# Up projection on fp16 halves with one scale taken in the mLSTM, the next unit's first products inside a unit, and down sums made by adding transfers

## The chip, the core and the metric

One Trainium2 chip, one of its cores. The core's engines are TensorE (PE; its weight loads are listed as PEld), VectorE (DVE), ScalarE (ACT), GpSimd (POOL) and SyncE (SP), which only issues transfers. The metric is the device time of one launch in microseconds (us). Each engine works through its own instructions in a fixed order; an instruction whose wait is not yet met holds everything behind it on that engine.

## The reference

One layer with two token mixers and a convolutional feed-forward block, in float32, for 1024 latent tokens of width 1024 and 256 context tokens:

```python
h  = modulate(rms_norm(x, norm1_w), sh1, sc1)           # and the same for ctx
q,k,v, mq,mk,mv,mo,mg, ga,gm = split(h @ w_in)
att = windowed_gqa(q, k, v, k_ctx, v_ctx, attn_sink)    # 16 heads, window 128, all context keys
ml  = mlstm_readout(mlstm_bidirectional(...), mo)       # 4 heads, chunks of 128, both directions
y   = sigmoid(ga) * (att @ w_branch_att) + sigmoid(gm) * (ml @ w_branch_ml)
x_mid = x + g1 * (y @ w_out)
u   = modulate(rms_norm(x_mid, norm2_w), sh2, sc2) @ w_up          # 1024 -> 2 * 2816
a,g = split(conv_b + depthwise conv of width 3 over tokens of u)
out = x_mid + g2 * ((silu(g) * a) @ w_down)                        # 2816 -> 1024
```

## The kernel before, in words

**Stages.** In the profiled execution the attention with its projections runs to about 560 us, the mLSTM (`stage_mlstm`) to about 955 us, the tail (`stage_tail`: branch products, the output projection `project`, the second norm, transposes, operand sums) to about 1208 us, the up projection in 22 units (`Units`, called from `stage_ffn`) to about 1636 us, and the down projection from there to the end.

**Halves.** A product of two float32 operands is made as three TensorE products of halves, high by high, high by low, low by high (`product`, L2023 to L2029; `mm3`, L163 to L165). `split_from` (L50) makes the halves: ACT copies the source to the high half (L47), DVE subtracts the high half from the source (L54, without a scale, or L56, with one). In the attention and mLSTM projections the halves are fp16 and the weights carry a scale; in the tail, up and down stages they are fp32r, 4 bytes an element. A TensorE instruction of the up stage multiplies a 128x128 block into a 128x512 bank of PSUM.

**The scheme with seven products.** The up and down projections use a Strassen-like scheme: seven products of quarter matrices instead of eight, with sums of quarters as operands. Of the activations `stage_tail` makes seven operands, `b11 b21 t2 t1 t3 b22 t4` (`put`). Of the weights, each unit j of 128 + 128 channels loads one 1 MB tile `ur` (`lead`), sums its quarters on DVE (`prep`, `prep2`) and splits them into pairs `r1 q1 q2 r2`. A product is 4 blocks x 3 = 12 TensorE instructions, a unit 7 products = 84, all 22 units 1848.

**Order of a unit.** `first_mm(j)` makes the two products that need only `r1`; `rest(j)` makes the other five and leaves two results `ua` and `ug`, which `conv_gate` (ACT and DVE) turns into a tile `a` of hidden channels and SP stores to `f_d` in DRAM. Unit j's operands are prepared during unit j-1.

**Sums for the down projection.** `weight_sums(k)` loads four 256 KB blocks of `w_down`, makes four subtractions on DVE and stores four blocks to `wt_d`: three of the eleven k in the tail (loads on ACT's queue, L1939, subtractions L1906), the others one per unit in the first half of the up stage. `hidden_sums(k)` runs in the second half: it loads a stored tile `fa` back, makes four operations on DVE with the present one and stores 512 KB each to `s1_d` and `s2_d`.

**The mLSTM's end.** `readout` squares the head's output on ACT, POOL makes the factor `rr` (L1520, and a power in L1521), DVE scales `hf` (L1524), TensorE transposes it (`mt`, L1532), and DVE multiplies by the gate (`mo`, L1534). The TensorE products that run meanwhile are those of the output gate (also named `mo`, operands `hH`/`hL` and `whqo`/`wlqo`). After that the branch product `yb` begins.

**Norm in the tail.** For each of the 8 row blocks of `x_mid`, `square` takes ACT squares, DVE adds them (L1873) and POOL raises them to a power (`rrx`, L1874); `scale` (L1877) multiplies the block, and transposes (`x2p`, L1913) read it.

**What sets the order.** Each engine's static order is laid down at build time from the program order, the tiles' dependences and a few `issue_after` marks. DMA issues stand in the order of the engine that issues them, with the same blocking rule.

## Time and profile before

| | |
|---|---|
| median of 3 runs (lowest, highest) | 1846.55 us (1845.82, 1847.97) |
| profiled execution, its time | 1849.14 us |
| its span on the core | 1847.4 us |
| mean granted TensorE clock | 0.988 |
| busy: PE, DVE, ACT, POOL | 1790.8, 1425.9, 1069.8, 508.3 us |
| moved | 342.47 MB, mean 185 GB/s |

"Busy" counts the union of an engine's instructions. A row of the timeline reads: start, duration, engine, line, operation, out<-in, shape, and in brackets how long the engine was idle before it and what ended that. A row of the table by stretches gives for each engine busy us and the number of instructions, then the granted clock, the DMA engines' mean busy share and GB/s.

### The profile page before, as it was taken

What the parts mean: (1) busy time and instruction counts of PE and PEld (TensorE: products, weight loads), DVE (VectorE), ACT (ScalarE), POOL (GpSimd) and SP (SyncE); (2) the same over time, 40 slices, a digit from 0 to 9 for tenths busy, and PEclk for the clock granted to TensorE, in tenths of its full rate; (3) what the DMA queues carried; (4) which work ended last, traced back from release to release, by engine and by line L of the source; (5) the groups of instructions that cost most, each with busy time, mean ns of one, the idle gap of its engine ahead of it and who ended that gap; (6) DMA issues with size and microseconds to landing.
All of it is one profiled execution on the core that took longest, in us unless ns stands there. A gap on an engine that the chain in (4) does not pass through costs nothing.

```text
span 1847.4 us, 27864 instructions
## 1 busy us (share of the span) xinstructions
PE 1790.8 (97%) x9207; PEld 1283.5 (69%) x9207; DVE 1425.9 (77%) x2864; ACT 1069.8 (58%) x2229; POOL 508.3 (28%) x747
## 2 busy tenths in 40 slices
PE   7989999999998899999999999999999999999999
PEld 3855555555554566656668887878888888888887
DVE  3858888888788686858687787698889898897665
ACT  4747877878787565645356462476444444465441
POOL 2467769587862530303010020000000000000000
PEclk9999999999999899999999999999999999999999
DMA  9747988888796625261359927322454544599751
GB/s 342 233 138 146 201 170 179 192 180 199 147 182 131 219 79 192 79 213 37 132 188 368 344 92 246 141 77 106 172 207 180 194 160 166 195 318 371 260 172 69
DMA packets 302193, 342.47 MB, mean 185 GB/s; under 512 B 176208, under 2 KB 200672, under 8 KB 299232
## 3 DMA queue, kind: packets, MB, share of 16 engines
q1 hardware_dynamic: 287648, 314.47, 56.3%
q10 hardware_dynamic: 14400, 26.22, 4.2%
q8 instruction: 72, 1.18, 0.3%
q14 instruction: 73, 0.60, 0.1%
HBM read 224.61 MB, written 76.16 MB: 163 GB/s over the span
## 4 chain that ended last, share of the span: by engine, by line
PE 78%; DVE 7%; DMA 4%; issue 3%; ACT 3%; POOL 3%; SPq 0%; ACTq 0%; DVEq 0%; POOLq 0%
PE g L706 8%; PE pq L706 6%; PE pa L2027 4%; PE pa L2029 4%; PE pa L2028 4%; PE po L706 3%; PE dx L2029 2%; PE dx L2027 2%; PE dx L2028 2%; PE pb L2027 2%; PE pb L2029 2%; PE pb L2028 2%; PE yb L2029 2%; PE yb L2027 2%; PE yb L2028 2%
## 5 line engine op out<-in xcount | busy, mean ns | idle before, releaser
L850 DVE CUSTOM_DVE_ANT_0 s<-s,maskA,nsink 128x640 f32<-128x640 f32 (+1 forms) x128 | 117.4, 917 | 65.5 <-PE s L845 65.0
L866 DVE TENSOR_TENSOR P<-s,P 128x640 f16<-128x640 f32 (+1 forms) x128 | 100.6, 786 | 1.0 <-ACT s L861 1.0
L860 ACT ACTIVATE P<-s,st 128x640 f16<-128x640 f32 (+1 forms) x128 | 98.2, 767 | 4.1
L706 PE MATMUL g<-hH,fh 128*128 128x512 f16 x256 | 97.1, 379 | 0.0
L706 PE MATMUL g<-hH,fl 128*128 128x512 f16 x256 | 97.0, 379 | 0.0
L706 PE MATMUL g<-hL,fh 128*128 128x512 f16 x256 | 97.0, 379 | 0.0
L861 ACT ACTIVATE s<-s,st 128x640 f32<-128x640 f32 (+1 forms) x128 | 93.8, 733 | 0.0
L706 PEld LDWEIGHTS <-hH 128*128 128x128 f16 x640 | 62.8, 99 | 37.3 <-issue 1.8
L858 ACT ACTIVATE st<-st,shift 128x1 f32<-128x1 f32 x128 | 37.6, 294 | 85.6 <-DVE st L850 84.8
L706 PE MATMUL pq<-wha,hH 128*128 128x384 f16 (+1 forms) x256 | 84.9, 332 | 0.1
L706 PE MATMUL pq<-wha,hL 128*128 128x384 f16 (+1 forms) x256 | 84.9, 332 | 0.0
L706 PE MATMUL pq<-wla,hH 128*128 128x384 f16 (+1 forms) x256 | 84.9, 332 | 0.0
L706 PEld LDWEIGHTS <-fh 128*128 128x128 f16 x512 | 49.2, 100 | 45.4
L2165 ACT ACTIVATE cv<-ua,vecT 128x1024 f32<-128x1024 f32 x22 | 27.4, 1246 | 84.9 <-DVE ua L2138 84.9
L1436 POOL TENSOR_SCALAR kwh<-k,gcall 128x128 fp32r<-128x128 f32 x72 | 32.5, 455 | 157.2 <-PE dC L164 53.9
L47 ACT ACTIVATE dfh<-drf 128x512 fp32r<-128x512 f32 x55 | 34.4, 628 | 59.3 <-PE dx L2028 26.5
L2027 PE MATMUL dx<-dwh,dfh 128*128 128x512 f32 (+1 forms) x176 | 68.3, 388 | 0.0
L2029 PE MATMUL dx<-dwh,dfl 128*128 128x512 f32 (+1 forms) x176 | 68.2, 388 | 0.0
L2028 PE MATMUL dx<-dwl,dfh 128*128 128x512 f32 (+1 forms) x176 | 68.2, 387 | 0.0
L54 DVE TENSOR_TENSOR dfl<-drf,dfh 128x512 fp32r<-128x512 f32 x55 | 37.6, 688 | 36.1 <-ACT dfh L47 36.1
L165 PE MATMUL kv<-whkv,hL 128*128 128x384 f16 x192 | 62.6, 326 | 0.0
L164 PE MATMUL kv<-wlkv,hH 128*128 128x384 f16 x192 | 62.6, 326 | 0.0
(691 smaller groups left out, 6249.9 us busy)
## 6 DMA issues: line engine op xcount, KB each, us to landing
ur<-in_w_up SPq DMA_DIRECT2D x22, 1024.0 KB
wmb<-in_w_modB SPq DMA_DIRECT2D x48, 256.0 KB
f_d<-cv SPq DMA_DIRECT2D x22, 512.0 KB
wm<-in_w_modA SPq DMA_DIRECT2D x16, 512.0 KB
fr<-in_w_g SPq DMA_DIRECT2D x32, 256.0 KB
drf<-fs_d SPq DMA_DIRECT2D x15, 512.0 KB
drw<-wt_d SPq DMA_DIRECT2D x14, 512.0 KB
w1b<-in_w_cx SPq DMA_DIRECT2D x16, 388.0 KB
```

Source lines behind the costliest of these rows:

```text
L54: rest = nc.vector.tensor_tensor(lo, src, whole, op=ALU.subtract)
L164: nc.tensor.matmul(ps, lh[:, ls], rl[:, rs], start=False, stop=False)
L165: nc.tensor.matmul(ps, ll[:, ls], rh[:, rs], start=False, stop=stop and i == n - 1)
L706: nc.tensor.matmul(self.ps, x, w, start=self.i == 0, stop=self.i == self.n - 1)
L850: nc.vector.tensor_tensor_reduce(e, e, self.mask, scale=self.ss[:, h : h + 1], scalar=nsink[:, hh : hh + 1], op0=ALU.add, op1=ALU.min, acc ...
L858: nc.scalar.activation(m, st4[:, 8 + h : 9 + h], AF.Identity, bias=shift)
L860: nc.scalar.activation(two[:, :W], e, AF.Exp, bias=m, scale=-1.0)
L861: nc.scalar.activation(e, e, AF.Exp, bias=m, scale=-1.0, accum_out=st4[:, 4 + h : 5 + h])
L866: nc.vector.tensor_tensor(two[:, W : 2 * W], self.e[h], two[:, :W], op=ALU.subtract)
L2027: nc.tensor.matmul(ps, lh, rh, start=start and i == 0, stop=False, skip_group_check=True)
L2028: nc.tensor.matmul(ps, lh, rl, start=False, stop=False, skip_group_check=True)
L2029: nc.tensor.matmul(ps, ll, rh, start=False, stop=stop and i == n - 1, skip_group_check=True)
```

## The change

Four things are done.

1. **fp16 halves.** The operands of the up products (`r1 q1 q2 r2` and the seven activation operands) become fp16, high and low half in one tile of the size that one fp32r half had (`xpair`, `pair4`, `pair2`). All weight pairs take one scale, `E.upf[:, 2:3]`, so the ACT copy has a per-partition scale and the DVE subtraction becomes the form of L56.
2. **The scale.** It is made from the sum of squares of the whole `w_up`. During the mLSTM, ACT issues 44 loads of 512 KB (128x1024, three buffers) and squares each with an accumulated sum (`up_load`, `up_square`); after the last head's output gate `up_scales` adds them up over partitions with one TensorE product, and takes reciprocals and powers on DVE and POOL. It also takes in `norm_factors` from the tail, and scales the modulation and the convolution weights in `m2` and `vecT` by the inverse factors.
3. **Order in a unit.** `rest(j, new, between)` makes the first two products of unit j+1 inside unit j, and calls `prep` and `prep2` of unit j+1 between products. A unit's weights are loaded two units ahead.
4. **Down sums.** `weight_sums` makes no DVE operation: POOL issues loads of `w_down` blocks that add into the tile on arrival, ten transfers per k, two k at a time, 110 in all; the three early sums in the tail and their ACT loads go. `hidden_sums` makes one DVE subtraction per unit; for the first eleven units SP writes three tiles to `s1_d` and `s2_d`, for the last eleven POOL adds to them in DRAM with two transfers each. Signs of the second eleven channel groups are flipped, and `finish` and the last additions subtract accordingly.

```diff
+    def up_load():
+        n = UP["load"]
+        if n < NUP:
+            raw = UP["raw"][n] = upp.tile([P, 4, 256], F32, tag="up", name=f"um{n}")
+            nc.scalar.dma_start(raw, A["w_up"][n // 2][:, 4 * (n % 2) : 4 * (n % 2) + 4])
+            UP["load"] += 1
+    def up_square(k):
+        for _ in range(k):
...
+                nc.scalar.activation(raw, raw, AF.Square, accum_out=E.up[:, n : n + 1])
+                UP["done"] += 1
+                up_load()
+    def up_scales():
+        f, g, m2, vecT = E.upf, E.upf[:, 8:], E.m2[:, 1:3], E.vecT
...
+        nc.tensor.matmul(pb[:, : NUP + 2], E.ones, E.up[:, : NUP + 2], start=True, stop=True)
+        nc.vector.tensor_reduce(f[:, 0:1], pb[:, :NUP], axis=AX.X, op=ALU.add)
+        nc.vector.tensor_scalar(g[:, 2:4], pb[:, NUP : NUP + 2], 1.0, 1e-30, op0=ALU.mult, op1=ALU.add)
+        nc.gpsimd.tensor_scalar(f[:, 1:2], f[:, 0:1], 2.0 ** -28, 1e-36, op0=ALU.mult, op1=ALU.add)
+        nc.gpsimd.tensor_tensor(f[:, 2:3], f[:, 1:2], expo[:, 0:1], op=ALU.pow)
+        nc.gpsimd.tensor_tensor(g[:, 4:5], g[:, 2:3], expo[:, 0:1], op=ALU.pow)
...
+        nc.gpsimd.tensor_tensor(f[:, 3:4], g[:, 4:5], expo[:, 0:1], op=ALU.pow)
+        nc.vector.reciprocal(f[:, 4:6], f[:, 2:4])
...
@@ proj_kv
+            if h and j >= NCB:
+                up_square(1)
@@ proj_q
+            if h:
+                up_square(2 if h == MLH - 1 else 1)
@@ proj_o
+                if h < MLH - 1:
+                    up_square(1)
+        if h == MLH - 1:
+            up_scales()
@@ stage_tail
-            B[m][k] = [x512(f"{m}{x}{k}", pool=homes[m]) for x in "hl"]
+            B[m][k] = xpair(f"{m}{k}", homes[m])
-    def weight_sums(k, a0, a1, b0, b1, eng=None):
...
-        sub(a0, a1, a0)
-        sub(a1, b1, a1)
-        sub(b1, b1, a0)
-        sub(b0, b0, b1)
...
+    def weight_sums(ks):
+        src = lambda n, o, k: A["w_dn"][n, :, o + k]
+        dma = nc.gpsimd.dma_start
...
+        for x, y, k in xy:
+            dma(x, src(0, 0, k))
+            dma(y, src(1, NK, k))
+        for x, y, k in xy:
+            dma(x, src(1, 0, k), accum_op=ALU.add)
+            dma(y, src(1, 0, k), accum_op=ALU.add)
+        for i, n, o in ((0, 1, NK), (1, 0, NK), (3, None, None)):
+            for x, y, k in xy:
+                dma(T[:, i, k], x)
+                if i == 0:
+                    dma(T[:, 2, k], y)
+            if n is not None:
+                for x, y, k in xy:
+                    dma(x, src(n, o, k), accum_op=ALU.add)
@@ class Units
-        split_from(self.nc, *p, src)
+        p = [self.v(t) for t in new(f"{nm}{j}")]
+        split_from(self.nc, *p, src, scale=self.scale)
-    def rest(self, j):
+    def rest(self, j, new=None, between=lambda i: None):
...
         product(nc, pb, op(q1, 0), B["t1"], True)
         copy_act(nc, ug[:, t1], pb)
+        between(0)
+        if new is not None:
...
+            product(nc, na, self.op(r1, 0), B["b11"], True)
...
         product(nc, pb, op(q2, 4), B["b22"], False)
         nc.vector.tensor_tensor(ua[:, t1], pb, ua[:, t1], op=ALU.add)
+        if new is not None:
...
+            product(nc, pc, self.op(r1, 4), B["b21"], True)
@@ stage_ffn
-    def hidden_sums(k, fb):
-        fa, o = [ur.tile([P, L], F32, tag="a", name=f"f{x}{k}") for x in "as"]
-        nc.sync.dma_start(fa, f_d[k * P : (k + 1) * P])
-        tt(o[:, t0], fa[:, t0], fa[:, t1], op=ALU.subtract)
...
+    def hidden_sums(j, a):
+        k = j % NK
+        u = E.x512(f"fu{j}", F32, 4)
+        tt(u, a[:, t1], a[:, t0], op=ALU.subtract)
...
+        if j < NK:
+            nc.sync.dma_start(s1_d[r, t1], a[:, t1])
+            nc.sync.dma_start(s1_d[r, t0], u)
+            nc.sync.dma_start(halves(s2_d), twice(u))
+        else:
+            nc.gpsimd.dma_start(halves(s1_d), twice(a[:, t1]), accum_op=ALU.add)
+            nc.gpsimd.dma_start(s2_d[r, t1], u, accum_op=ALU.add)
```

**ACT in the mLSTM**, where head 1's keys (`k`) and values (`VH`) are copied out of the projection's result `kv`. Before (L112 squares weights of the next projection, L1550 issues loads of branch weights):

```order
L47 ACTIVATE k_9_8589<-kv_9_8590,wfw_ml_8492 128x128
L47 ACTIVATE VH_9_8616<-kv_9_8590,wfw_ml_8492 128x256
L1550 DMA s_ba_0_9023<-in_w_ba 128x512 x2
L112 ACTIVATE wjw_ml_0_9682,wqw_ml_9681<-wrw_ml_0_9673 128x768
L47 ACTIVATE k_8_8638<-kv_8_8639,wfw_ml_8492 128x128
L47 ACTIVATE VH_8_8665<-kv_8_8639,wfw_ml_8492 128x256
L1550 DMA s_ba_1_9024<-in_w_ba 128x512 x2
L112 ACTIVATE wjw_ml_1_9684,wqw_ml_9681<-wrw_ml_1_9675 128x768
L112 ACTIVATE wjw_ml_2_9686,wqw_ml_9681<-wrw_ml_2_9677 128x768
```

After:

```order
L1584 DMA um_8698<-in_w_up 128x1024
L1592 ACTIVATE um_8463,upq<-um_8463 128x1024
L1592 ACTIVATE um_8646,upq<-um_8646 128x1024
L47 ACTIVATE k_9_8612<-kv_9_8613,wfw_ml_8515 128x128
L47 ACTIVATE VH_9_8639<-kv_9_8613,wfw_ml_8515 128x256
L1584 DMA um_8734<-in_w_up 128x1024
L1584 DMA um_8770<-in_w_up 128x1024
L47 ACTIVATE k_8_8664<-kv_8_8665,wfw_ml_8515 128x128
L47 ACTIVATE VH_8_8691<-kv_8_8665,wfw_ml_8515 128x256
L1592 ACTIVATE um_8698,upq<-um_8698 128x1024
L1592 ACTIVATE um_8734,upq<-um_8734 128x1024
L1584 DMA um_8822<-in_w_up 128x1024
```

Between the copies stand now loads of `w_up` (L1584) and squares of 128x1024 (L1592); a load stands behind the square that frees its buffer.

**DVE at the mLSTM's end.** `hf` is scaled by `rr` for the two halves of the last head, four tiles each, then come the gate products `mo` and the first low halves of the branch product. Before:

```order
L1524 TENSOR_SCALAR hf_11521<-hf_11521,rr_0_12050 128x256 x4
L1524 TENSOR_SCALAR hf_11521<-hf_11521,rr_1_12065 128x256 x4
L1534 SCALAR_TENSOR_TENSOR mo_0_0_12085<-mt_0_0_12080,mlw,sg_0_11944 128x512
L1534 SCALAR_TENSOR_TENSOR mo_0_1_12093<-mt_0_1_12088,mlw,sg_0_11944 128x512
L54 TENSOR_TENSOR bawl_0_12182<-bawr_12179,bawh_0_12181 128x512
L54 TENSOR_TENSOR baal_0_12228<-baar_12225,baah_0_12227 128x512
L54 TENSOR_TENSOR bawl_1_12184<-bawr_12179,bawh_1_12183 128x512
```

After:

```order
L1533 TENSOR_SCALAR hf_11658<-hf_11658,rr_0_12207 128x256 x4
L1606 TENSOR_REDUCE upf<-upq 128x1
L1607 TENSOR_SCALAR upf<-upq 128x2
L1533 TENSOR_SCALAR hf_11658<-hf_11658,rr_1_12222 128x256 x2
L1615 RECIPROCAL upf<-upf 128x2
L1533 TENSOR_SCALAR hf_11658<-hf_11658,rr_1_12222 128x256 x2
L1543 SCALAR_TENSOR_TENSOR mo_0_0_12242<-mt_0_0_12237,mlw,sg_0_12081 128x512
L1543 SCALAR_TENSOR_TENSOR mo_0_1_12250<-mt_0_1_12245,mlw,sg_0_12081 128x512
L54 TENSOR_TENSOR bawl_0_12340<-bawr_12337,bawh_0_12339 128x512
```

The reduction over the TensorE product `upq` (L1606, L1607) stands between the two groups of four, and the reciprocal of the factors (L1615) in the middle of the second group. On TensorE `upq` stands behind the last product of the output gate.

**POOL at the same place**, from the second half's `rr` on. Before, the first products of the tail follow at once:

```order
L1520 TENSOR_SCALAR rr_1_12065<-rr_1_12065 128x4
L1521 TENSOR_TENSOR rr_1_12065<-rr_1_12065,expo 128x4
L1782 TENSOR_TENSOR sgm_13024<-sgm_13024,y_13026 128x512
L1782 TENSOR_TENSOR sgm_13028<-sgm_13028,y_13030 128x512
L1782 TENSOR_TENSOR sgm_13032<-sgm_13032,y_13034 128x512
```

After:

```order
L1529 TENSOR_SCALAR rr_1_12222<-rr_1_12222 128x4
L1608 TENSOR_SCALAR upf<-upf 128x1
L1530 TENSOR_TENSOR rr_1_12222<-rr_1_12222,expo 128x4
L1609 TENSOR_TENSOR upf<-upf,expo 128x1
L1610 TENSOR_TENSOR upf<-upf,expo 128x1
L1611 TENSOR_TENSOR upf<-upf 128x1
L1612 TENSOR_SCALAR upf<-upf 128x1
L1613 TENSOR_SCALAR upf<-upf 128x1
L1614 TENSOR_TENSOR upf<-upf,expo 128x1
L1617 TENSOR_SCALAR m_70<-m_70,upf 128x16
L1616 TENSOR_TENSOR upf<-upf 128x1
L1619 TENSOR_SCALAR vecT<-vecT,upf 128x132
```

The small operations of `up_scales` follow the last `rr`, and the first of them (L1608) stands ahead of that half's power (L1530).

**POOL in the tail.** The eight powers `rrx` of the norm stood behind one another with nothing between. Before, the last five:

```order
L1874 TENSOR_TENSOR rrx_14085<-rrx_14085,expo 128x1
L1874 TENSOR_TENSOR rrx_13827<-rrx_13827,expo 128x1
L1874 TENSOR_TENSOR rrx_13857<-rrx_13857,expo 128x1
L1874 TENSOR_TENSOR rrx_13887<-rrx_13887,expo 128x1
L1874 TENSOR_TENSOR rrx_13933<-rrx_13933,expo 128x1
```

After, from the seventh to the eighth of them:

```order
L1941 TENSOR_TENSOR rrx_14049<-rrx_14049,expo 128x1
L2014 DMA wy_15341<-in_w_dn 128x512
L2020 DMA wt_d<-wx_15049 128x512
L2013 DMA wx_15342<-in_w_dn 128x512
L2020 DMA wt_d<-wx_15051 128x512
L2014 DMA wy_15343<-in_w_dn 128x512
L2025 DMA wx_15049<-in_w_dn 128x512
L2016 DMA wx_15340<-in_w_dn 128x512
L2025 DMA wx_15051<-in_w_dn 128x512
L2017 DMA wy_15341<-in_w_dn 128x512
L2020 DMA wt_d<-wx_15049 128x512
L1941 TENSOR_TENSOR rrx_14079<-rrx_14079,expo 128x1
```

Here `wx` and `wy` are the tiles of `weight_sums`: L2013 and L2014 load, L2016, L2017 and L2025 load with an addition, L2020 and L2022 store. Six such transfers stand ahead of the sixth power, nine between the sixth and the seventh, ten between the seventh and the eighth.

162 lines of the change are left out of this document (100 added, 62 removed).

## The prediction

> **What bounds the kernel now.** I read the page's busy shares first, then the stretches of 10 to 100 us, then the waits and the timelines of the places that the change touches. The first row is the page's, the others are from the table by stretches.
>
> ```profile
> PE 1790.8 (97%) x9207; PEld 1283.5 (69%) x9207; DVE 1425.9 (77%) x2864; ACT 1069.8 (58%) x2229; POOL 508.3 (28%) x747
> ...
> 850.00:900.00 50.00, 49.58 (x299) 30.18 (x298) 33.76 (x85) 28.11 (x65) 6.62 (x16) 1.00 0.29 101
> 900.00:950.00 50.00, 49.66 (x299) 34.44 (x298) 39.32 (x135) 24.19 (x61) 10.66 (x23) 1.00 0.32 109
> 950.00:1000.00 50.00, 46.60 (x211) 35.85 (x210) 37.30 (x65) 30.49 (x59) 1.21 (x2) 1.00 0.93 339
> ...
> 1400.00:1500.00 100.00, 100.00 (x443) 82.79 (x442) 88.19 (x106) 47.97 (x58) 0.00 (x0) 1.00 0.48 179
> ```
>
> TensorE sets the pace from the mLSTM on, and in the up stage without a gap: 100.00 of 100 us, DVE at 88 and ACT at 48. So an engine's relief there is worth nothing, a shorter TensorE stream is worth all of it, and whatever delays TensorE before the up stage costs its whole length.
>
> **Term 1, the fp16 stream.** The starts of fp32r instructions in one unit, and of fp16 ones of the same shape in the last output gate, both at full clock:
>
> ```profile
> 1500.20 0.39 PE L2027 MATMUL pa<-b11h,r1h 128*128 128x512 f32 x1
> ...
> 1512.44 0.39 PE L2027 MATMUL pb<-b22h,q2h 128*128 128x512 f32 x1
> ```
>
> ```profile
> 945.25 0.38 PE L163 MATMUL mo<-hH,whqo 128*128 128x512 f16 x1
> ...
> 954.32 0.38 PE L163 MATMUL mo<-hH,whqo 128*128 128x512 f16 x1
> ```
>
> 12.24 us over 54 instructions is 226.7 ns; 9.07 us over 42 is 216.0 ns. The up stage has 1848 of them: 1848 x 10.7 ns = **-19.8 us**. The Trainium skill (page "TensorE: Matmul & The Clock Gate", section "Wait — 56ns, not 53.3ns?") lets the moving columns over 2.4 GHz and about 2.5 ns set the spacing, some 216 ns at 512 columns. For fp16 the rows agree. Taken for every type, it would leave this term at nothing; the 226.7 ns of this trace contradict that.
>
> Not all instructions can use it. At the stage's start DVE is the bound, since it still makes the activation operands:
>
> ```profile
> 1220.00:1230.00 10.00, 9.76 (x44) 7.51 (x42) 10.00 (x27) 10.00 (x26) 0.00 (x0) 1.00 0.00 0
> 1230.00:1240.00 10.00, 10.00 (x45) 8.30 (x45) 10.00 (x21) 6.38 (x13) 0.00 (x0) 1.00 0.33 107
> ```
>
> DVE is busy for 20.00 of 20 us until about 1240, and 1240 - 1208 = 32 us of the stage, some 141 instructions, may gain nothing: 141 x 10.7 ns = **+1.5**. After that DVE must follow a unit of 84 x 216 ns = 18.1 us instead of 19.0. It worked 0.88 x 19.0 = 16.8. The second half of the units loses three of four subtractions, the first half four weight subtractions; each splitting in the form with a scale costs a little more:
>
> ```profile
> L2182 DVE TENSOR_TENSOR fs<-fa 128x512 f32<-128x512 f32 x11 | 7.5, 685 | 1.6 <-DMA fa<-f_d 1.6
> ...
> L54 DVE TENSOR_TENSOR q2l<-s,q2h 128x1024 fp32r<-128x1024 f32 x21 | 25.7, 1225 | 15.8 <-ACT q2h L47 15.8
> ```
>
> ```profile
> L56 DVE SCALAR_TENSOR_TENSOR wlqo<-wrw_mlqo,wfw_mlqo,whqo x12: 1006/1008/1010, 691.6 to 880.3; 128x768 f16<-128x768 f32 x12
> ```
>
> Three subtractions at some 0.6 us of engine time are 1.8 less; the split of 128x1024 goes from 1225 to about 1008 x 4/3 = 1344 ns, times three and a half, 0.4 more: 16.8 - 1.4 = 15.4 us, 85% of 18.1. Nothing is added for DVE. That the next unit's first two products stand inside a unit changes no count, and with TensorE at 100.00 there is no gap it could close.
>
> **Term 2, the scale at the mLSTM's end.** The chain before, on DVE, POOL and TensorE:
>
> ```profile
> 951.53 1.14 DVE L1524 TENSOR_SCALAR hf<-hf,rr 128x256 f32<-128x256 f32 x4 [0.43 <-POOL rr L1521]
> 955.60 1.41 DVE L1534 SCALAR_TENSOR_TENSOR mo<-mt,mlw,sg 128x512 f32<-128x512 f32 x2 [2.93 <-PE mt L1532]
> ```
>
> ```profile
> 950.21 0.19 POOL L1520 TENSOR_SCALAR rr<-rr 128x4 f32<-128x4 f32 x1 [0.28 <-ACT rj L1519]
> 950.49 1.01 POOL L1521 TENSOR_TENSOR rr<-rr,expo 128x4 f32<-128x4 f32 x1
> ```
>
> ```profile
> 954.97 2.10 PE L1532 MATMUL mt<-ident,hf 128*128 128x128 f32 x16
> 959.54 0.50 PE L2027 MATMUL yb<-baah,bawh 128*128 128x512 f32 x1 [2.48 <-ACT bawh L47]
> ```
>
> DVE had the scaling done at 952.7, while TensorE still had the output gate to finish. Now the reduction stands between the two groups of scalings and waits for `upq`, which TensorE reaches only behind that gate, at 955.0. POOL's first operation waits for this, with the second half's power (1.01) behind it, then the chain of three single-column powers and four small operations up to the reciprocal, on which DVE's last two scalings, `mo` and the low halves of the branch product wait. A single-column power takes 0.55 (the row at 1188.61 below); for a small POOL operation I put the 0.2 of L1520. From 955.0: product and two DVE operations with hand-overs, to 955.8; 0.2 + 1.0 to 957.0; 3 x 0.55 + 3 x 0.2, with some 0.1 each for seven hand-overs, to 959.9; reciprocal and two scalings, to 960.6. `mo` began at 955.60, so everything on DVE behind it moves by **+4.9**, and TensorE waits for it: `yb` needs the low halves made after `mo`. Bounds: 2.5, if the low halves' lateness is met by the 2.48 us that `yb` waits for ACT anyway, and 7, if hand-overs are double.
>
> A gap of this length has a second price in this trace. The waits of TensorE name one of 8.4 us, and the stretch around it has a granted clock below 1:
>
> ```profile
> PE dC L163 <- DVE C L1442: 8.4, 1, 8.4
> ```
>
> ```profile
> 600.00:650.00 50.00, 40.98 (x219) 28.04 (x218) 33.31 (x72) 27.47 (x76) 28.50 (x56) 0.83 0.66 209
> ```
>
> 0.17 x 50 = 8.5 us of clock lost, half of it while TensorE stood. Here transposes fall into the gap; I take **+1.7**, between 0 and 4.3.
>
> **Term 3, the squares.** One square of this size costs, from the startup's rows:
>
> ```profile
> L392 ACT ACTIVATE xj<-x x5: 1036/1052/1056, 11.2 to 47.0; 128x1024 bf16<-128x1024 f32 x5
> L392 ACT ACTIVATION_READ_ACCUMULATOR xj<-x x5: 185/186/198, 12.1 to 48.0; 128x1 f32 x5
> ```
>
> 44 x 1.24 = 54.5 us on ACT in about 300 us, where its share is 24 to 28 of 50: it goes to some 70%. Most lie beside TensorE, since ACT there waits for TensorE, not the other way:
>
> ```profile
> ACT nm L1487 <- PE i L165: 30.0, 28, 2.6
> ```
>
> What is not covered is a copy of a projection's bank, or of a state inside a core, that comes 1.24 us late: of 12 squares inside cores, all of it is 12 x 1.24 = 15 us, none is 0. The 44 loads are issued on ACT's own queue and wait for the square that frees the buffer, which is on the same engine, so they add no wait of their own; the squares wait for the transfers, at a DMA share of 0.3. I take **+3**, nearer to nothing, since TensorE has some 300 instructions in 50 us with other heads' work between.
>
> **Term 4, POOL's queue in the tail.** Before, the powers of the norm have POOL to themselves. Fifth and eighth, and who waits:
>
> ```profile
> 1188.61 0.55 POOL L1874 TENSOR_TENSOR rrx<-rrx,expo 128x1 f32<-128x1 f32 x1 [4.40 <-DVE rrx L1873]
> ...
> 1211.69 2.47 POOL L1874 TENSOR_TENSOR rrx<-rrx,expo 128x1 f32<-128x1 f32 x1 [7.88 <-DVE rrx L1873]
> ```
>
> ```profile
> 1215.04 0.75 DVE L1877 TENSOR_SCALAR acc<-acc,rrx 128x1024 f32<-128x1024 f32 x1 [1.29 <-DMA xm_d<-acc]
> 1215.85 1.20 PE L1913 MATMUL x2p<-ident,acc 128*128 128x128 f32 x9 [1.38 <-DVE acc L1877]
> ```
>
> Now 25 transfers stand between these two powers, and through the tile `wx` six of them follow one another by landing: load, add, store, add, store, add. They have 1211.69 - 1188.61 = 23.1 us, 3.85 each, and 0.9 us of slack (the scaling waits for a transfer until 1215.04, the power ends at 1214.16). How long one takes is not in the trace for POOL's queue. From below, a 512 KB store, issued when the sum at 1186.45 is done and landed before 1190.38, takes 3.2 us:
>
> ```profile
> 1186.45 0.69 DVE L1861 TENSOR_TENSOR acc<-op,acc 128x512 f32<-128x512 f32 x1 [1.32 <-PE op L165]
> 1190.38 0.75 DVE L1877 TENSOR_SCALAR acc<-acc,rrx 128x1024 f32<-128x1024 f32 x1 [0.85 <-DMA xm_d<-acc]
> ```
>
> From above, a load of 256 KB at a DMA share of 0.75 took 7 us, from its issue to the subtraction that waited for it:
>
> ```profile
> 1148.27 0.84 ACTq L1939 DMA_DIRECT2D w<-in_w_dn  x2
> ```
>
> ```profile
> 1155.27 2.15 DVE L1906 TENSOR_TENSOR w<-w,w 128x512 f32<-128x512 f32 x3 [1.21 <-DMA w<-in_w_dn]
> ```
>
> So 0 to 6 x 7 - 23.1 - 0.9 = 18 us. The share at 1190 to 1210 was 0.13, so the unloaded row is nearer; I take **+2**. The Trainium skill (page "SBUF — State Buffer", section "SBUF: two separate sides") warns that transfers issued by GpSimd cannot get their descriptors written while DVE runs an operation in a mode that takes the port pair the two share. By that rule landings would lengthen with DVE's work, which is the rival on POOL's queue below; the eighth power's 2.47 instead of 0.55 us, with DVE nearly without a pause beside it, may be of that kind, but no row here shows a transfer on that queue.
>
> **The sum** is -19.8 + 1.5 + 4.9 + 1.7 + 3 + 2 = **-6.7 us** on the profiled execution's 1849.14, so 1842.4; that execution lies 2.6 above the median of 1846.55, and from the median the forecast is 1839.8, say **1840**.
>
> **Rivals.** *All that is added is hidden*: `yb`'s wait takes up most of term 2, terms 3 and 4 are nothing, and -19.8 + 1.5 + 2.5 remain: 1831. For it speaks that TensorE has gaps of 3.4 us in 950 to 1000 already; against it the static order, in which the powers are behind the last gate product. *The squares are on the path*: +15 instead of +3, 1852; a core's states are a chain through ACT, but with gaps of up to 2.6 us. *Slower by POOL's queue*: at 7 us a landing the eighth power comes 18 us late, TensorE has no other work than the first unit's products, and the time is 1840 + 16 = 1856; it makes the kernel slower from about 5.5 us a landing on (6 x 5.5 - 24 = 9, that is 7 more than taken, so no gain is left). *The change doesn't give the shorter stream*: the units turn out to be paced by DVE, or by POOL's additions holding the tiles `a`; then term 1 is near -8 and the time about 1852.
>
> **How the numbers follow.** Forecast 0.45 (1835 to 1845), all hidden 0.18, squares 0.14, POOL's queue 0.13, no shorter stream 0.10. A measurement of this kernel can tell from no change what differs by over 0.2%, 3.7 us: faster is below 1842.9, slower above 1850.2. Faster holds three quarters of the forecast and "all hidden" nearly whole, and odd parts of the others: 0.56; no change 0.20; slower 0.24. The range goes from 1829, a little under "all hidden", to 1855, short of POOL's queue at its full price.
>
> **What would show it.** Right: in the up stage starts 216 ns apart, TensorE still at 100%, the stage about 18 us shorter than from 1208 to 1636; behind the last gate product a gap of some 7 us that ends on DVE or POOL; ACT 10 to 13 us busier in each 50 between 650 and 950 with TensorE's idle time up by about 3; the eighth `rrx` at most 2 us later against the transposes before it. Wrong: a gap of over 5 us of TensorE before `x2p` that ends on POOL's power, TensorE waiting for ACT's copies in the cores, or for the splits in the units.

## The result and the profile after

The changed kernel takes **1902.4 us** (median of 4 runs, 1899.9 to 1904.9), the kernel before on the same chip 1846.7: a ratio of 1.030, 95% interval 1.028 to 1.032. Slower, by 56 us; forecast were 1840 us and a range of 1829 to 1855.

The profiled execution has a span of 1903.1 us against 1847.4, at a mean granted clock of 0.971 against 0.988. Its busy shares:

```profile
PE 1794.7 (94%) x9209; PEld 1132.0 (59%) x9209; DVE 1393.3 (73%) x2801; ACT 1121.5 (59%) x2321; POOL 616.1 (32%) x894
```

TensorE is busy nearly as long as before (1790.8), so the 56 us are waiting for the most part. The starts of three products cut the span into stages; "forecast" is what the prediction's terms add to each:

| stage | before | after | difference | forecast |
|---|---|---|---|---|
| start to first `yb` (end of the mLSTM) | 959.5 | 1002.4 | +42.9 | +9.6 |
| tail, to the first up product `pa` | 249.0 | 250.2 | +1.2 | 0 |
| up stage, to the first `dx` | 423.6 | 434.4 | +10.8 | -16.3 |
| down stage | 215.3 | 216.1 | +0.8 | 0 |

So there are two errors: the mLSTM by 33 us, the up stage by 27. In both, the table by stretches of the kernel after shows TensorE with gaps, and with the gaps mostly a higher share of the DMA engines than before (columns as in the prediction: PE, PEld, DVE, ACT, POOL busy, clock, DMA share, GB/s). Here are three stretches of the mLSTM, then four of the up stage:

```profile
700.00:760.00 60.00, 50.94 (x262) 33.01 (x261) 33.72 (x82) 31.27 (x69) 6.78 (x16) 0.86 0.66 222
820.00:880.00 60.00, 49.40 (x252) 34.65 (x250) 36.51 (x104) 25.92 (x59) 13.57 (x30) 0.86 0.71 230
...
940.00:1000.00 60.00, 50.28 (x294) 33.97 (x291) 47.40 (x153) 24.73 (x62) 16.39 (x36) 0.94 0.47 158
```

```profile
1240.00:1300.00 60.00, 49.52 (x232) 27.87 (x231) 46.44 (x99) 35.69 (x77) 31.23 (x43) 0.91 0.95 246
1300.00:1420.00 120.00, 109.53 (x494) 48.45 (x492) 106.99 (x125) 65.61 (x76) 42.79 (x62) 0.99 0.97 291
1420.00:1500.00 80.00, 80.00 (x373) 36.30 (x371) 70.34 (x80) 42.12 (x49) 0.56 (x1) 1.00 0.42 147
1500.00:1600.00 100.00, 100.00 (x465) 45.31 (x464) 86.01 (x95) 53.57 (x63) 9.95 (x10) 1.00 0.52 129
```

The same first two stretches before:

```profile
700.00:760.00 60.00, 59.46 (x367) 40.96 (x366) 41.98 (x133) 32.30 (x79) 15.27 (x44) 1.00 0.32 109
820.00:880.00 60.00, 56.83 (x341) 39.45 (x342) 50.62 (x158) 31.27 (x69) 18.17 (x45) 0.97 0.23 75
```

In the first of them TensorE begins 262 products instead of 367, at a clock of 0.86. Later, from 1420 on, the forecast stands: 100.00 of 100 us with 465 instructions instead of 443, that is 215 ns each.

**Who holds the mLSTM.** Its waits name small, scattered things for TensorE (the longest is 6.2 us in all); it is ACT's waits that have long single entries (total, times, longest, from 640 to 1000):

```profile
ACT sh L47 <- issue: 9.1, 1, 9.1
...
ACT CH L47 <- DMA um<-in_w_up: 8.0, 1, 8.0
ACT sh L47 <- DMA t_at_d<-t_at: 7.7, 1, 7.7
```

`sh` and `CH` are the high halves of scores and states, on which a core's next products wait. ACT's timeline there, in the kernel after:

```profile
724.09 0.19 ACT L1592 ACTIVATION_READ_ACCUMULATOR um<-um 128x1 f32 x1
731.38 1.98 ACTq L1559 DMA_DIRECT2D s_ba<-in_w_ba  x4
733.40 0.63 ACT L47 ACTIVATE sh<-ub 128x512 fp32r<-128x512 f32 x1 [9.12 <-issue]
...
742.73 0.33 ACTq L1584 DMA_DIRECT2D um<-in_w_up  x1
746.00 2.32 ACTq L1567 DMA_DIRECT2D t_at<-attT_d  x4
748.36 0.73 ACT L47 ACTIVATE CH<-C 128x258 fp32r<-128x258 f32 x2 [7.96 <-DMA um<-in_w_up]
```

ACT has nothing to do from 724.3 to 731.4, since the next item in its order is a transfer that may not be issued yet, and `sh` stands behind it. `s_ba` and `t_at` belong to a job that the prediction didn't mention. `branch_sums`, called during the mLSTM, loads four blocks of branch weights or attention outputs at a time (L1559, L1567, issued by ACT), DVE forms operand sums, SP stores them. The program's rows of ACT's queue show what such an issue waits for:

```
1060 L1584 DMA um_9645<-in_w_up 128x1024 [waits DMAHW2_49,Activation_49]
1061 L1559 DMA s_ba_0_9090<-in_w_ba 128x512 [waits DMAHW3_49,DMAHW7_49,DMAHW0_49,DVE_49]
1062 L1559 DMA s_ba_0_9090<-in_w_ba 128x512 [waits DMAHW4_49]
1063 L1559 DMA s_ba_1_9091<-in_w_ba 128x512 [waits DMAHW6_49,DMAHW5_49,DMAHW1_49]
1064 L1559 DMA s_ba_1_9091<-in_w_ba 128x512
1065 L47 ACTIVATE sh_1_1_9145<-ub_1_1_8564 128x512 [waits DVE_49]
```

The counters DMAHW0 to DMAHW7 are eight that all transfers of SP and ACT share, and a wait names a counter for an earlier transfer, whichever engine issued that. Two kinds of wait stand under these names. In row 1061, DMAHW7 and DMAHW0 are the stores of the block of branch sums before, out of the same buffers: DVE made the last of these sums at 728.04, SP issued the stores from 724.88 to 728.38, and ACT's load followed at 731.38. The wait of 9.12 us is one for buffers. A load of a square, such as row 1060, needs only the square before it for its data; 28 of the 44 wait for a counter besides, 19 of them for a transfer that SP issued. ACT's idle time directly ahead of the transfers it issues, added up from its timeline from 600 to 1000 (without those of `sga`, which belong to the tail), is 33 us, before 11. Some 30 of the 33 stand ahead of loads for the branch sums, under 4 ahead of loads for the squares.

In this order the branch sums' loads have also moved: before, they stood mostly among the copies of the keys; now they stand behind the queries `qh`, in front of the core's `sh` and `CH`.

The Trainium skill (page "DMA: Bandwidth & Descriptors", section "Anatomy of one DMA — SWDGE (gpsimd) path") says that DMA engines do not wait on semaphores; a wait happens on the issuing sequencer before dispatch. The trace agrees: the 9.12 and 7.96 us above are such waits on ACT's queue.

**Who holds the up stage.** At its start TensorE waits once for 9.3 us, where it waited 1.4, and POOL's order shows why (fifth, seventh and eighth power of the norm, with the last transfers before the eighth):

```profile
1231.43 0.55 POOL L1941 TENSOR_TENSOR rrx<-rrx,expo 128x1 f32<-128x1 f32 x1 [4.26 <-DVE rrx L1940]
...
1250.19 2.59 POOL L1941 TENSOR_TENSOR rrx<-rrx,expo 128x1 f32<-128x1 f32 x1
...
1261.22 0.87 POOL L2025 DMA_DIRECT2D wx<-in_w_dn  x1 [1.86 <-DMA wt_d<-wx]
1264.93 0.86 POOL L2017 DMA_DIRECT2D wy<-in_w_dn  x1 [2.84 <-issue]
...
1266.05 0.90 POOL L1941 TENSOR_TENSOR rrx<-rrx,expo 128x1 f32<-128x1 f32 x1
```

```profile
PE x2p L1980 <- DVE acc L1944: 9.3, 1, 9.3
```

From fifth to eighth power are 34.6 us instead of 23.1. After that, with the DMA engines at 0.95 to 0.97, the units' own weights `ur` come late. ACT waits for them before it splits them, and its copies of TensorE's banks stand behind that. ACT's waits from 1240 to 1430:

```profile
ACT r L47 <- DMA ur<-in_w_up: 29.2, 8, 7.3
```

At the stage's end DVE stands for 7.48 us at 1662.3 to 1669.8 before a subtraction of the down stage, whose buffer a POOL transfer still reads.

### The profile page after: what moved, and what is told of

The parts are those of the page before. It is cut to its first block, busy times and chain, and to the rows that moved or that the text cites. A ratio compares the mean times of both kernels' runs of the same rounds, so it can differ in the third digit from the quotient of the medians.

```text
span 1903.1 us, 27891 instructions
## 1 busy us (share of the span) xinstructions
PE 1794.7 (94%) x9209; PEld 1132.0 (59%) x9209; DVE 1393.3 (73%) x2801; ACT 1121.5 (59%) x2321; POOL 616.1 (32%) x894
## 4 chain that ended last, share of the span: by engine, by line
PE 71%; DMA 10%; DVE 9%; POOL 4%; issue 2%; ACT 2%; SPq 0%; ACTq 0%; DVEq 0%; POOLq 0%
PE g L707 8%; PE pq L707 6%; PE po L707 3%; PE pa L2104 3%; PE pa L2103 3%; PE pa L2105 3%; PE yb L2103 2%; PE yb L2105 2%; PE yb L2104 2%; PE dx L2103 2%; PE dx L2105 2%; PE dx L2104 2%; DMA ur<-in_w_up 2%; PE kv L164 2%; PE kv L165 2%
## 5 line engine op out<-in xcount | busy, mean ns | idle before, releaser
L1445 POOL TENSOR_SCALAR kwh<-k,gcall 128x128 fp32r<-128x128 f32 x72 | 37.1, 518 | 185.4 <-PE dC L164 78.9
L2279 POOL DMA_DIRECT2D fs_d<-cv x11 | 12.1, 1102 | 248.2 <-DVE cv L2259 248.2
L2103 PE MATMUL pa<-t,q 128*128 128x512 f16 x176 | 68.4, 389 | 10.2 <-ACT ua L47 10.2
L2104 PEld LDWEIGHTS <-q 128*128 128x128 f16 x352 | 34.8, 99 | 56.8 <-issue 17.0
L2105 PE MATMUL pa<-t,q 128*128 128x512 f16 x176 | 68.5, 389 | 0.0
L2104 PE MATMUL pa<-t,q 128*128 128x512 f16 x176 | 68.3, 388 | 0.0
```

Of the source, the lines that this page charges most:

```text
L1445: E.kw = nc.gpsimd.tensor_scalar(kh, ks[c], wk, 1.0, op0=ALU.mult, op1=ALU.mult)
L2103: nc.tensor.matmul(ps, lh, rh, start=start and i == 0, stop=False, skip_group_check=True)
L2104: nc.tensor.matmul(ps, lh, rl, start=False, stop=False, skip_group_check=True)
L2105: nc.tensor.matmul(ps, ll, rh, start=False, stop=stop and i == n - 1, skip_group_check=True)
```

## The experiments

All are edits of the changed kernel unless said otherwise; the ratio is to the kernel before on the same chip (1844.7 to 1846.9 us there), with its 95% interval. "yb" is the start of the first branch product, "up" the length of the up stage. Both are taken from one profiled execution each, which can lie up to 6 us from the median of its kernel (e3 6.1 above, e1 5.7 above, e4 2.2 below), so a few us between these columns and the medians mean nothing.

| run | median us | ratio | yb | up |
|---|---|---|---|---|
| before | 1846.7 | 1 | 959.5 | 423.6 |
| after | 1902.4 | 1.030 (1.028 to 1.032) | 1002.4 | 434.4 |
| e1 no squares, no loads | 1857.3 | 1.006 (1.004 to 1.008) | 958.6 | 434.7 |
| e7 squares without loads | 1859.0 | 1.007 (1.005 to 1.009) | 956.6 | 430.0 |
| e8 loads without squares | 1869.4 | 1.011 (1.009 to 1.014) | 966.8 | 433.1 |
| e2 branch sums among the keys | 1888.4 | 1.024 (1.021 to 1.026) | 989.2 | 429.1 |
| e6 branch sums' loads on SP | 1883.9 | 1.020 (1.019 to 1.022) | 981.9 | 432.6 |
| e13 both | 1880.4 | 1.019 (1.017 to 1.021) | 975.8 | 433.9 |
| e15 squares' loads on SP | 1867.4 | 1.013 (1.011 to 1.014) | 965.1 | 431.1 |
| e3 scale made later | 1895.8 | 1.027 (1.025 to 1.030) | 999.2 | 432.8 |
| e5 down sums of before | 1879.9 | 1.017 (1.014 to 1.020) | 1007.1 | 409.1 |
| e4 transfers behind the 8th power | 1895.3 | 1.028 (1.026 to 1.030) | 1002.2 | 423.4 |
| e11 `fu` in another pool | 1904.3 | 1.032 (1.030 to 1.034) | 1001.5 | 433.3 |
| e9 4 squares, sums of before | **1835.1** | 0.994 (0.992 to 0.995) | 955.2 | 409.2 |
| e10 as e9, sums spread on POOL | 1887.9 | 1.023 (1.020 to 1.026) | 956.7 | 440.8 |
| e12 as e9, unit order of before | 1847.9 | 1.001 (1.000 to 1.002) | 957.1 | 421.9 |
| e16 as e9, all 44 squares | 1846.1 | 1.000 (0.999 to 1.001) | 964.1 | 409.7 |

### The squares: e1, e7, e8

e1 issues no load and makes no square; the 44 sums are a constant 1. e7 makes all 44 squares, but of the first three tiles over and over. e8 loads everything and squares eight columns of each piece.

```diff
 # e1
+    nc.gpsimd.memset(E.up, 1.0)
-        if n < NUP:
+        if False and n < NUP:
...
 # e7, in up_load and up_square
-        if n < NUP:
+        if n < 3:
...
-                raw = UP["raw"].pop(n)
+                raw = UP["raw"][n % 3]
 # e8
-                nc.scalar.activation(raw, raw, AF.Square, accum_out=E.up[:, n : n + 1])
+                nc.scalar.activation(raw[:, 0, 0:8], raw[:, 0, 0:8], AF.Square, accum_out=E.up[:, n : n + 1])
...
```

> The changed kernel without the 44 loads of w_up and the 44 squares in the mLSTM; the sums that they would give are set to a constant (1.0 each, about what they come to), and everything from the TensorE product on stays. Theory A (what the squares do is to move the loads for the branch sums on ACT's queue behind the projections, into the cores): the mLSTM gets its old length back but for the chain at its end, the branch products begin at about 966 us instead of 1002, the time is about 1866. Theory B (the 44 squares stretch ACT by their own 54 us): the same, 1866. Rival C (the 43 us before the branch products have little to do with the squares, but with the scale's chain at the end and the clock after it): they begin at 990 or later, the time is 1890 or more.

> The changed kernel with all 44 squares of 128x1024 on ACT, but only three loads of w_up: the squares take the same three tiles again and again (the scale then is another one). ACT's order has the branch sums' loads among the copies of keys again, as before the change. Theory of ACT's time (54 us more of work on ACT): the branch products begin at 985 us or later, the time is 1885 or more. Theory of the transfers (22 MB more, and the order that they bring about): 965 to 972, the time is 1864 to 1872.

> The changed kernel with all 44 loads of w_up, but each square over 8 columns instead of 1024 (the scale is corrected by the factor 128), so ACT has some 45 us less work. Branch sums' loads stand partly behind the queries again on ACT's queue. Theory of the transfers: the branch products begin at 985 us or later, the time is 1885 or more. Theory of ACT's time: 965 to 972, the time is 1864 to 1872.

Without both, 45.1 us are gone and `yb` stands where it stood before. That is 8 us earlier than both theories of e1 had it, so what they allowed for the scale's chain isn't there (more on that under e3). e7 refutes the theory of ACT's time, and e8 comes out at the numbers that were given for that very theory, so neither theory holds alone. The parts do not add up: squares alone cost 1.7 us, which lies within the spread of the runs, loads alone 12.1, both 45.1. In e7 TensorE loses almost nothing in the stretch with the most squares, though ACT is nearly full:

```profile
640.00:760.00 120.00, 117.14 (x718) 80.00 (x718) 93.11 (x299) 111.52 (x249) 34.15 (x93) 1.00 0.33 111
```

111.52 of 120 us of ACT, so the forecast of ACT's time was right, and it left ACT little reserve. In e8, ACT's idle time ahead of its issues is 30 us, nearly the 33 of the kernel after, but there ACT has no squares to catch up on. That is one reading of why both together cost three times the sum of each; no run shows it alone. The other is the order: in e7 the branch sums' loads stand among the keys again, in e8 most of them do, and this place is worth 14.0 us, as e2 shows next.

### Where the loads stand: e2, e6, e13, e15

```diff
 # e2: branch_sums() called from the loop over keys, as before, and not after the queries
...
+                if 3 <= done < 3 + (3, 4, 3)[h - 1]:
+                    branch_sums()
...
-            for _ in range((3, 4, 3)[h]):
-                branch_sums()
 # e6 (and e13, with e2's edit): L1559 and L1567
-                nc.scalar.dma_start(o, src)
+                nc.sync.dma_start(o, src)
 # e15: the squares' loads; the branch sums then fall among the keys by themselves
-            nc.scalar.dma_start(raw, A["w_up"][n // 2][:, 4 * (n % 2) : 4 * (n % 2) + 4])
+            nc.sync.dma_start(raw, A["w_up"][n // 2][:, 4 * (n % 2) : 4 * (n % 2) + 4])
```

> The changed kernel with all its squares, but the branch sums are called one by one inside the projection of keys and values, so that on ACT their loads stand among the copies of keys and values again instead of behind the queries, ahead of the core's state copies. Theory A (place of these loads): the branch products begin at 966 to 975 us, the time is 1866 to 1876. Theory B (ACT's own time and the loads' transfers): they begin at 990 to 1002 as before, the time is 1890 to 1902.

> The changed kernel with the 40 loads of the branch sums issued from SP's queue instead of ACT's; squares and loads of w_up as they are. Theory A (ACT stands still because those loads wait, on its own queue, for a buffer that a store has yet to leave): the branch products begin at 970 to 980 us instead of 1002, the time is 1868 to 1880. Theory B2 (the loads of w_up slow the other transfers, whichever queue issues them): 985 or later, 1885 or more; SP's queue holds the weights and the cores' matrices behind the same waits.

> The branch sums' loads are issued among the keys again and on SP's queue, so that ACT issues only the 44 loads that it squares; both earlier edits together, which alone gave 14 and 18.5 us. Theory (the squares' 45 us are ACT's own queue: transfers issued there that wait for a buffer hold ACT's copies, at whatever place they stand): yb begins by 970, ACT has no idle stretch over 4 us between 640 and 950 that ends on a branch sum's tile, time 1868 to 1874. Rival (the 22 MB in the same stretch make every other transfer late, the weights above all): yb not before 980, TensorE waits for DVE's low halves of weights (wlqo, wlkv) by 5 us or more, time 1880 or above.

> Only the 44 loads of w_up are issued on SP's queue instead of ACT's; the branch sums' loads then stand on ACT among the keys, as in the kernel before. SP holds the stores and the weights' loads behind a load that waits for a square. Theory (ACT's queue): ACT's copies in the cores are not held, yb at 965 to 975, time 1865 to 1877. Rival (transfers are late whoever issues them): yb at 985 or later, with weights that come late because SP stands on a load that waits for a square, time 1885 or above.

e2 gave back 14.0 us, e6 18.5, both together (e13) 22.0, where adding them would give 32.5. e2 and e6 fall between their two theories. e13 meets neither either: `yb` at 975.8 lies between their bounds, though the time is just inside the rival's. ACT still stands, now ahead of the squares' loads themselves. The timeline of ACT in e13:

```profile
706.07 0.40 ACT L47 ACTIVATE CH<-C 128x258 fp32r<-128x258 f32 x1
710.62 0.33 ACTq L1587 DMA_DIRECT2D um<-in_w_up  x1
711.00 0.37 ACT L47 ACTIVATE k<-kv,wfw_ml 128x128 f32<-128x128 f32 x1 [4.53 <-DMA t_at<-attT_d]
```

The load of a square waits for a branch-sum transfer that SP issued, with which it shares no data. That is the wait of the shared counter, which moving the other transfers away doesn't remove (in e13, 36 of the 44 loads wait for a counter). ACT's idle time ahead of its issues is still 20 us, all of it ahead of loads of `um`. DVE's waits for branch-sum loads add up to 51 us in e13 (30 in the kernel after), two of them:

```profile
DVE s_bm L1563 <- DMA s_bm<-in_w_bm: 19.2, 3, 7.3
DVE t_at L1571 <- DMA t_at<-attT_d: 14.6, 3, 5.9
```

e15 moves the 44 loads only, and gives back 35.0 us of 45.1, as the theory of ACT's queue had it (yb 965.1, 1867.4). Since the branch sums fall among the keys with it, e2 is the kernel to compare for the issuer alone: 21.0 us lie between them, though the squares, too, stand at other places in the two. ACT's idle time ahead of issues falls to 7 us, less than before the change. The same volume is moved, in the first stretch at a higher share (0.80). The Trainium skill (page "DMA: Bandwidth & Descriptors", section "Issuing engines are not separate DMA queues") says that transfers of all issuing engines run on the same 16 DMA engines, and that issuing from several saves only the time on the sequencer. Here the time on ACT's sequencer was a wait with ACT's copies behind it, so that the choice of the issuer decided about tens of us.

What is left is 10.1 us above e1, 6.5 of them at `yb`. It shows most from 700 to 760, where squares wait for their transfers at that share; the rows of e15, the stretch and ACT's wait (640 to 1000):

```profile
700.00:760.00 60.00, 52.97 (x312) 37.88 (x309) 36.09 (x109) 43.01 (x99) 13.74 (x37) 0.91 0.80 258
```

```profile
ACT um L1592 <- DMA um<-in_w_up: 14.2, 7, 5.3
```

### The scale at the end of the mLSTM: e3

```diff
-        if h == MLH - 1:
-            up_scales()
 # behind the last turn of the cores
+            up_scales()
```

> The changed kernel with the chain of the scale called behind the last head's transposes instead of behind its output gate, so that on DVE the scalings of hf and the first gate products stand ahead of the reduction and the reciprocal. Theory (the chain's wait is on the path with 5 to 7 us): the branch products begin 4 to 7 us sooner, the time is 1895 to 1898. Rival (the wait for ACT's first half of the branch weights ends the gap anyway): less than 2 us sooner, the time is 1900 to 1903.

`yb` begins 3.2 us earlier, between the two theories; the median is 6.6 less, as the theory had it. The profiled executions differ by 3.0 us only, and the runs of the two kernels overlap (1893.7 to 1901.9 and 1899.9 to 1904.9), so more than some 3 us isn't shown. On POOL the chain is in the kernel after as the prediction laid it out; POOL's timeline:

```profile
990.32 0.19 POOL L1608 TENSOR_SCALAR upf<-upf 128x1 f32<-128x1 f32 x1 [0.90 <-DVE upf L1607]
990.59 1.02 POOL L1530 TENSOR_TENSOR rr<-rr,expo 128x4 f32<-128x4 f32 x1
...
993.71 0.56 POOL L1614 TENSOR_TENSOR upf<-upf,expo 128x1 f32<-128x1 f32 x1
```

From 990.3 to 994.3 are 4.0 us; laid out were 955.8 to 959.9, 4.1. But the chain reaches `yb` by another path than the prediction had. TensorE's transposes wait for `hf`, 3.7 us in three pieces. After them `yb` doesn't wait for low halves made behind `mo`, but for ACT's copy `bawh`, and ACT waits for branch weights that SP loads only behind the store of `mo`. The rows of SP, ACT and TensorE in the kernel after:

```profile
995.67 0.99 SPq L1544 DMA_DIRECT2D mlT_d<-mo  x2
996.76 0.40 SPq L1801 DMA_DIRECT2D bawr<-in_w_ba  x1
...
1001.74 1.15 ACT L47 ACTIVATE bawh<-bawr 128x512 fp32r<-128x512 f32 x2 [8.91 <-DMA bawr<-in_w_ba]
...
1002.42 0.80 PE L2103 MATMUL yb<-baah,bawh 128*128 128x512 f32 x1 [5.60 <-ACT bawh L47]
```

In e3 the store goes out 4.6 us sooner and the load 3.6, and `yb` still waits 5.60 us for `bawh`. In e1, where the chain stands behind the gate too but SP issues these loads ahead of the store, `yb` waits 2.32 us for `bawh`, as before (2.48), and begins no later than before.

### The down sums: e5, e4, e11

e5 takes the functions `weight_sums` and `hidden_sums` of before, with their signs and their ACT loads in the tail. e4 lets the first transfers be issued only behind the eighth power. e11 moves a tile.

```diff
 # e4
...
+            with tc.issue_after(E.pw.ins):
-            weight_sums([k for k in (j, j + 1) if k < NK])
+                weight_sums([k for k in (j, j + 1) if k < NK])
 # e11
-        u = E.x512(f"fu{j}", F32, 4)
+        u = E.x512(f"fu{j}", F32, 3)
```

> The changed kernel with the down sums of before: subtractions on DVE, transfers on SP and ACT, no additions by transfer. Theory D (POOL's 132 transfers fill the transfer engines from 1230 to 1410 us and hold the eighth power, the units' weights and a tile of the down projection): no gap ahead of the transposes of over 2 us, transfer share in the first third of the up stage at 0.5 to 0.6 instead of 0.98, TensorE without gaps there, the up stage from its first product to the first of the down projection about 408 us instead of 434, the time about 1876. Rival E (DVE with the splits in the form with a scale paces the units): the stage stays above 420 us, the time is 1888 or more.

> The changed kernel with POOL's transfers for the down sums put behind the eighth power of the norm on POOL's queue. Theory (the 9.3 us ahead of the transposes are this queue's, and the rest of the up stage's loss is the full transfer engines' and comes later as before): the gap goes, the time is 1888 to 1895. Rival (the same transfers then crowd into fewer units, and what is won is lost there): 1898 or more.

> The changed kernel with the tile fu, which POOL's adding transfers read, in a pool of tiles that the down projection's first halves do not use. Theory (DVE stood 7.5 us at 1662 because the half dwl took a slot that such a transfer still read): the stop and TensorE's 5.5 us behind it go, the time is 1893 to 1898. Rival (the stop was for the weights drw, landing late): it stays, 1900 or more.

With the old sums the time falls by 22.5 us, and the up stage by 25.3 to 409.1. Theory D holds, with the time 4 us longer than it gave. This is where the adding transfers belong on the bill: they free DVE, which was hardly a bound (in e5 from 1320 to 1420, DVE has 99.84 of 100 us of work and TensorE 99.58), and fill the DMA engines, which then are one. e4 takes away the gap at `x2p` (9.3 to 1.4 us) and 11.0 us of the stage, 7.1 of the median. e11 removes the 7.48 us in which DVE stood at the end, so the buffer was the cause, and yet the time stays (1904.3), against the theory: ACT then waits there for loads of the down projection's operands (`drf` up to 6.3 us, `drw` 4.9). In e11's table of queues from 1640 to 1700 (packets, MB, share of the 16 engines' time) the adding transfers are queue q0, SP's plain ones q1:

```profile
q1 hardware_dynamic: 3667, 9.73, 46.3%
q0 software_dynamic: 1441, 2.75, 31.4%
```

31.4 / 2.75 = 11.4% a MB against 4.8: a MB added into DRAM from POOL's queue took 2.4 times the DMA time of a plain one of SP there. What the queue does to this and what the addition does, no run here separates.

### What the fp16 stream brings alone: e9, e10, e12, e16

e9 has the old down sums, the scale behind the last turn, and takes the scale from 4 of the 44 pieces of `w_up`, times 11; the other 40 pieces are left out of it. e10 has e9's scale and e11's place for `fu`, and puts the sums on POOL again, one k per two units, each behind its unit's hidden tile. e12 is e9 with the unit order of before and the weights loaded one unit ahead. e16 is e9 with all 44 pieces, loaded by SP; nothing is left out.

```diff
 # e9, beside e5's and e3's edits (e10 and e12 have it too)
-    NUP = 2 * NFC
+    NUP = 4
...
 # e10, in weight_sums(ks, late)
+            for t in (x, y):
+                nc.gpsimd.tensor_scalar(t[:, 0:1], late[:, 0:1], 1.0, None, op0=ALU.mult)
...
 # e12
-    def rest(self, j, new=None, between=lambda i: None):
+    def rest(self, j):
...
 # e16, against e9, with e15's edit
-    NUP = 4
+    NUP = 2 * NFC
```

> fp16 halves and the order in a unit as in the change, the down sums of before (subtractions on DVE), the scale from 4 of the 44 pieces of w_up (each a half of one unit's weights) instead of all, its chain behind the last transposes. If the squares' 45 us, the down sums' 25 us and the chain's 3 us are separate causes, they add up: 1902 - 45 - 25 - 3 = 1829, and 1826 to 1836 in all, faster than before. If they share causes (late transfers), the time is 1840 to 1850.

> As in the run with few squares (scale from 4 of 44 pieces, chain behind the last transposes), but the down sums by adding transfers on POOL as in the change, spread out: one k for every two units, each begun only when that unit's hidden tile is there, so none stands among the norm's powers; fu in the other pool. Theory (the transfers were too many at a time, not too slow): transfer share at 0.6 to 0.8 all through the up stage, no gaps, the stage 404 to 412 us long, the time 1828 to 1836. Rival (adding transfers on POOL's queue hold the units at any rate): 418 us or more, 1842 or more.

> The run with few squares and the old down sums, with the units' old order: first two products at a unit's start, preparation behind it, weights loaded one unit ahead. Forecast's step (the order within a unit is worth nothing): 1833 to 1838. Rival (with units of 18.1 us and DVE at 95% the old order leaves TensorE waiting): 1840 or more.

> The down sums of before, the scale made after the turn, and the scale taken from all 44 pieces again, with their loads on SP's queue: nothing of the computation is left out. If the parts add: 1835.1 (the run with four pieces) plus the 10.1 us by which the squares with their loads on SP stood above the kernel without squares (1867.4 against 1857.3) less about 1 for the four pieces = 1844 (1841 to 1848), about the kernel before. Rival (the transfers of the squares cost less where the branch sums' loads and the early w_down loads are as before): below 1841. Rival (SP, which holds the weights and stores, is the bound): above 1850.

**e9** is faster than both kernels: 1835.1, 11.6 below before, with the up stage at 409.2. It came out 6 above what the parts add up to (1829), inside the range given for separate causes. e9's rows from the table by stretches, and e12's:

```profile
1300.00:1400.00 100.00, 98.47 (x457) 44.46 (x456) 96.98 (x116) 53.41 (x63) 0.00 (x0) 1.00 0.61 206
...
1500.00:1600.00 100.00, 100.00 (x465) 45.34 (x464) 92.09 (x110) 52.97 (x68) 0.00 (x0) 1.00 0.56 199
```

```profile
1500.00:1600.00 100.00, 96.95 (x445) 43.37 (x444) 88.74 (x106) 50.89 (x62) 0.00 (x0) 1.00 0.50 180
```

```profile
PE pa L2092 <- ACT ua L47: 9.1, 9, 3.4
```

**e12** has fp16 without the new order, and nearly nothing is left of the gain: up 421.9, total 1847.9. The rival was right that the old order leaves TensorE waiting, but it had put that down to DVE. At 216 ns an instruction a unit is short enough that the next unit's first product waits for ACT to copy the last bank (the wait above, e12, 1230 to 1630); with the next unit's products inside a unit, 465 instructions fit into 100 us instead of 445.

**e10** ends where its rival had it (1887.9, up 440.8). It shows that the adding transfers can be spread so that the DMA engines have room (0.70 to 0.75, TensorE 100.00 of 100 from 1350 to 1550), and that POOL's one queue is then the next bound. A step of the chain takes 4.5 us; POOL's timeline in e10:

```profile
1498.59 0.56 POOL L2021 DMA_DIRECT2D wt_d<-wx  x1 [3.74 <-DMA wx<-in_w_dn]
1503.06 0.87 POOL L2026 DMA_DIRECT2D wx<-in_w_dn  x1 [3.92 <-DMA wt_d<-wx]
1507.68 0.56 POOL L2021 DMA_DIRECT2D wt_d<-wx  x1 [3.75 <-DMA wx<-in_w_dn]
```

A k takes some 37 us, two units 36; the hidden sums' transfers stand behind it in the same queue, DVE waits for their buffer, and TensorE for DVE (1400 to the end):

```profile
PE pa L2104 <- DVE ug L2216: 16.5, 2, 15.5
PE dy L2105 <- DVE dwl L54: 14.3, 1, 14.3
```

**e16** adds up as written: 1844 expected, 1846.1 measured, no difference from before (0.9998, 0.9987 to 1.0010). Measuring the scale from all of `w_up` in the mLSTM, with SP issuing the loads, costs 11.0 us over e9, and eats the gain of the fp16 stream.

## Why the prediction was wrong

**Term 3, the squares: +3 forecast, 45.1 measured.** The step that failed is the sentence that the 44 loads "wait for the square that frees the buffer, which is on the same engine, so they add no wait of their own". Ahead of these loads ACT indeed stands for under 4 us in the kernel after. But they are not alone in the queue. They and their squares moved the branch sums' loads in front of the cores' copies, where ACT stands some 30 us for those loads' buffers and counters; and through the shared counters their own wait is for transfers of SP as well (e13). Which of the two waits weighs more, no run separates. The 15 us given as the upper bound was a bound on ACT's work, not on its queue. ACT's work was priced rightly (e7: 1.7). Of the 45.1 us, 14.0 go with the old place of the branch sums' loads (e2), 35.0 when SP issues the squares' loads and that place comes back (e15), and 10.1 stay with them there. The clock adds to it: 0.86 in two of the stretches with gaps.

The trace of before had such waits. In the view that gave the prediction its "gaps of up to 2.6 us" stand two further rows, waits of ACT's copies with an issue for the branch sums right ahead of the copy:

```profile
ACT qh L47 <- DMA s_bm<-in_w_bm: 5.1, 1, 5.1
...
ACT k L47 <- DMA t_at_d<-t_at: 4.6, 1, 4.6
```

**Term 4, POOL's queue: +2 forecast, 7.1 measured (e4).** The rival named this mechanism, with its place and its price: 18 us late at 7 us a landing, slower from 5.5 on. Landings had a median of 6.9 us for the loads and 5.1 for the stores of `wx`; the eighth power came 34.6 us after the fifth, 11.5 more than before, the gap before `x2p` was 9.3, and keeping the queue free of it gave 11.0 us of the stage (e4). The step that failed is the choice between the bounds: the DMA share of 0.13 was read from before, where the very transfers that raise it were not yet there. After, it is 0.95. Whether DVE's port use lengthened the landings, as the Trainium skill's page "SBUF — State Buffer" (section "SBUF: two separate sides") warns, no run here separates from the full DMA engines.

**The down sums had no term beyond the tail.** They were counted as relief of DVE; their price for the DMA engines in the up stage, where ACT's splits then wait for `ur` and TensorE for ACT, was not asked for. All of the down sums' change costs 22.5 us (e5), of which e4's later start of the transfers gets back 7.1.

**Term 1, the fp16 stream: right in size for one instruction.** It was 215 ns as forecast (216), but the up stage of the kernel after is 10.8 us longer all the same. In e9 it is 14.4 us shorter, forecast 18.3. So in e9 5.4 of the 19.8 us could not be used, not 1.5: DVE's bound doesn't end at 1240, from 1300 to 1400 it still has 96.98 of 100 us of work and TensorE 98.47. (e9 keeps the subtractions of before, of which the forecast had taken some off DVE.)

**The order in a unit "could close no gap"** was argued from a trace with fp32r instructions. It is worth 12.7 us with fp16 ones (e12 against e9): nearly all of term 1 depends on it. Without it the rival "no shorter stream" would have come near with its time, but not with its reason: TensorE waits for ACT's copies there, not for DVE or POOL.

**Term 2, the chain: length right, path wrong.** It was 4.0 us on POOL as laid out. The step that failed is that "`yb` needs the low halves made after `mo`": `yb` waited 5.60 us for ACT's `bawh`, whose weights SP loaded behind the store of `mo`. The effect at `yb` was 3.2 us in e3's profile and none in e1, where those loads stand ahead of the store (forecast 4.9, and 1.7 for the clock).

As a check on the bill: 1902.4 - 45.1 (squares) - 22.5 (down sums) - 6.6 (scale later) = 1828.2, that is 18.5 below before, and e9, which keeps four squares, has 1835.1. The 7 us between them are not more than the spread of the single differences.

## What to carry to other kernels

Price a transfer that is added to an engine's queue by what stands behind it there, and read from the program's rows which buffers and counters the issues there wait for, those of other jobs too: an issue that waits holds the engine's compute work, even if its own engine frees its buffer. A DMA share read from the kernel before is no ground for transfer times in a stretch into which the change puts transfers. A gap that a saturated trace doesn't show can open once the instructions become shorter, so steps of one change that look worthless alone should be priced together.
